# Queries and output gate of a hybrid block as block products, and where the branch gates' tiles run

## The chip, the cores and the metric

The kernel runs on one core of a Trainium2 chip. The core has TensorE for matrix products, VectorE and ScalarE for elementwise work, GpSimd (POOL) for elementwise work and for issuing transfers, SyncE (SP) for issuing transfers, and 16 DMA engines. Products land in PSUM, eight banks of 128 partitions x 512 float32. The metric is the device time of the core in microseconds; the time before is the median of three runs.

## The reference

One layer of a hybrid block on x of 512 tokens x 1024 features, in float32. Cut to what matters:

```python
h = rmsnorm(x, norm_mix_g)
gq, gk, gv, gr, glr, fq, fk, fv, ff, g_gla, g_fox = jnp.split(h @ w_in, IN_OFFSETS, axis=-1)
o_gla = gla_chunked(gq, gk, gv, log_a)                       # 4 heads, chunks of 64
o_gla = rmsnorm(o_gla, gla_out_norm_g) * jax.nn.silu(gr)     # output gate, 512 columns
o_fox = fox_attention(rmsnorm(fq), rmsnorm(fk), fv, log_f)   # 8 heads, queries 512 columns
y = sigmoid(g_gla + gate_b[0]) * (o_gla @ w_gla_branch) + sigmoid(g_fox + gate_b[1]) * (o_fox @ w_fox_branch)
x = x + y @ w_out
a, val = jnp.split(rmsnorm(x, norm_ffn_g) @ w_up, 2, axis=-1)
out = rmsnorm(x + (gelu(causal_dwconv(a)) * val) @ w_down)
```

Queries fq, keys fk, values fv and the output gate gr have 512 columns each, the gates g_gla (first) and g_fox (second) 1024 each.

## The kernel before

**Products.** Each float32 operand is split into a high part, rounded by ScalarE, and a low part, the difference, by VectorE (lines 293 and 294, one weight piece of 128 x 1024 each). `mm3` (lines 327 to 330) makes one product out of three on TensorE: high x high, high x low, low x high. Weights come in pieces of 512 KB, in the order of a list, `recipes`. `piece()` takes the next one; splits run three pieces ahead of TensorE (three buffers), loads up to four further, into places named raw, rawz, rawp or zr with two buffers each. SP issues the plain loads. A piece that is a sum of weight blocks is loaded first, and then another block is added to it by an accumulating transfer that POOL issues; `behind(n, ...)` names the split behind which a load, a sum or an addition is issued. Additions ("add") go into a place whose piece has just been split; "sum" is issued behind a one-column copy on POOL, `tick` (line 309).

**Block products.** Keys and values together (`fox_kv`, lines 737 to 787), the output projection and the MLP use a 2 x 2 block scheme with seven products for eight. `PAIR` (line 78) is its order: for each product p of 5, 1, 3, 6, 2, 7, 4 two pieces, each of 12 matmuls of 512 columns (two token tiles x two feature blocks x three). The left half of the result is the keys, the right half the values. `pair_done` combines the banks with ScalarE and VectorE, squares the keys and normalises them. The sums of activations that it multiplies with are made once (`pair_sums`, `pair_split`).

**Stages.** After a first stage (gated attention's q and k) come the gated attention's values. Then its small products are made; between them `fill(n)` takes n steps of a work list, so that TensorE has something while VectorE and ScalarE work. In this kernel the list holds `fox_q` (16 steps of 6 matmuls, token form) and `fox_kv` (28 steps of 6). `normalise` (lines 861 to 876) scales the gated attention's output by its norm, and transposes it, with a fill in each round.

Then comes the softmax attention. Its work list is `gates`: four tiles of the output gate gr (`zr`) and eight of the first branch gate (`zg`), each 24 matmuls in eight steps of three (`gate_tile`, line 927). `FRONT` and `RUNS` (lines 41 to 49) spread these 96 steps by hand between logits, transposes (t), values (v) and preparations of keys and queries (k).

Behind the attention the output gate's sigmoid, the product with it and with the gain, and the split into `ogh` and `ogl` run on ScalarE, GpSimd and VectorE (lines 1130 to 1139). The merge loop (lines 1142 to 1180) takes for each of eight column blocks c one tile of the second branch gate (`zf`, two blocks ahead, `GAHEAD`) and one branch piece: 12 matmuls for the gated branch, 12 for the attention branch. VectorE multiplies both with their gates, GpSimd adds them, and VectorE and ScalarE make the operands of the output projection's block products. Two pieces of that projection are split early and held (`HELD`). The MLP follows, and the second norm.

Beside this the weights of the down projection are combined in DRAM: copies (`COPY_AT`, issued on SP) and accumulating transfers (`ADD_AT`, on POOL) are hung behind chosen splits.

The instructions of each engine go in an order that a scheduler sets at build time: by program order, but an instruction whose operands are not ready by its estimate lets a later one pass; `issue_after` keeps an order.

## Time and profile before

| what | us |
|---|---|
| median of three runs (688.61, 690.53, 691.12) | 690.53 |
| the profiled execution | 688.75 |
| its span, first to last instruction | 687.0 |
| TensorE busy in the span | 680.2 |
| VectorE busy | 547.8 |
| ScalarE busy | 430.9 |
| GpSimd busy | 136.3 |

Busy time counts the instructions of an engine, not the time in which it waits; matmuls overlap, so their start-to-start distance tells more than their duration. In the rows of the profile PE is TensorE's matmuls, PEld its weight loads, DVE VectorE, ACT ScalarE, POOL GpSimd. A timeline row gives start, duration, engine, line, operation, output<-inputs, shape and count; a bracket gives the idle time before it and what ended it. A group row ends with busy time and mean duration in ns. In a row of transfers the last number is the median time from issue to landing in us.

### The profile page before, as it was taken

To read this page: it belongs to the slowest core of one execution; us is meant where nothing else is said; L and a number is where in the kernel's file an instruction comes from. 1 tells how busy PE (TensorE), PEld (TensorE's weight loads), DVE (VectorE), ACT (ScalarE), POOL (GpSimd) and SP (SyncE) were. 2 spreads that over 40 slices of the span, in tenths; PEclk is the share of its full clock that TensorE was granted. 3 is DMA by queue.
4 is the path that set the end of the run, shared out by engine and by line. 5 is a ranking of instruction groups with operands and counts; after the bars stand their busy time and mean duration, and the time that the engine had idled before them with its cause. 6 is when DMAs were issued, how large, how long until landed. Compare 5 with 4: busy or idle time off the path is not lost.

```text
span 687.0 us, 10636 instructions
## 1 busy us (share of the span) xinstructions
PE 680.2 (99%) x3875; PEld 585.4 (85%) x3875; DVE 547.8 (80%) x856; ACT 430.9 (63%) x698; POOL 136.3 (20%) x196
## 2 busy tenths in 40 slices
...
DMA  8769488989765489967975898999999988866643
GB/s 310 270 192 306 99 273 221 311 196 217 178 140 122 119 248 199 281 147 213 213 253 133 158 211 210 228 228 223 196 201 214 204 202 254 268 209 173 196 139 122
DMA packets 46184, 142.23 MB, mean 207 GB/s; under 512 B 5396, under 2 KB 9388, under 8 KB 46004
## 3 DMA queue, kind: packets, MB, share of 16 engines
q1 hardware_dynamic: 31156, 92.98, 40.3%
q0 software_dynamic: 11808, 43.52, 35.8%
...
## 4 chain that ended last, share of the span: by engine, by line
PE 99%; ACT 0%; issue 0%; DVE 0%; ACTq 0%
PE ps_mm L328 21%; PE ps_mm L330 20%; PE ps_mm L329 20%; PE ps_wide L1463 8%; PE ps_wide L328 5%; PE ps_wide L329 5%; PE ps_wide L330 5%; PE ps_wide L1465 4%; PE ps_lg L1042 1%; PE ps_lg L983 1%; PE ps_pt L1017 1%; PE ps_mm L490 1%; PE ps_ax L328 1%; PE ps_ax L330 1%; PE ps_ax L329 1%; PE ps_ax L378 1%
## 5 line engine op out<-in xcount | busy, mean ns | idle before, releaser
L293 ACT CAST wh<-rawx 128x1024 fp32r<-128x1024 f32 x75 | 76.0, 1013 | 61.5 <-PE ps_mm L329 30.9
L328 PE MATMUL ps_mm<-xw,wh 128*128 128x512 f32 (+1 forms) x320 | 109.4, 342 | 0.2 <-ACT wh L293 0.2
L329 PE MATMUL ps_mm<-xw,wh 128*128 128x512 f32 (+1 forms) x320 | 107.8, 337 | 0.0
L330 PE MATMUL ps_mm<-xw,wl 128*128 128x512 f32 (+1 forms) x320 | 107.6, 337 | 0.0
L294 DVE TENSOR_TENSOR wl<-rawx,wh 128x1024 fp32r<-128x1024 f32 x75 | 88.3, 1179 | 13.8 <-ACT wh L293 13.8
L294 DVE TENSOR_TENSOR wl<-raw,wh 128x1024 fp32r<-128x1024 f32 x58 | 74.6, 1287 | 9.7 <-ACT wh L293 9.4
L293 ACT CAST wh<-raw 128x1024 fp32r<-128x1024 f32 x58 | 60.7, 1049 | 32.0 <-PE ps_mm L329 20.2
L328 PEld LDWEIGHTS ps_mm<-xw,wh 128*128 128x128 f32 x320 | 60.8, 190 | 7.8 <-issue 1.2
L330 PEld LDWEIGHTS ps_mm<-xw,wl 128*128 128x128 f32 x320 | 60.8, 190 | 6.5
L329 PEld LDWEIGHTS ps_mm<-xw,wh 128*128 128x128 f32 x320 | 60.8, 190 | 5.9 <-DVE xw L1252 0.2
L294 DVE TENSOR_TENSOR wl<-rawz,wh 128x1024 fp32r<-128x1024 f32 x31 | 39.2, 1266 | 16.7 <-ACT wh L293 16.4
L1463 PE MATMUL ps_wide<-xo,wh 128*128 128x512 f32 x192 | 48.1, 392 | 0.0
L301 POOL DMA_DIRECT2D rawx<-in_wu_dram x30 | 25.9, 865 | 104.6 <-DVE wl L294 68.6
L328 PE MATMUL ps_mm<-xc,wh 128*128 128x256 f32 (+1 forms) x136 | 45.1, 332 | 0.0
L329 PE MATMUL ps_mm<-xc,wh 128*128 128x256 f32 (+1 forms) x136 | 44.6, 328 | 0.0
L330 PE MATMUL ps_mm<-xc,wl 128*128 128x256 f32 (+1 forms) x136 | 44.5, 327 | 0.0
L293 ACT CAST wh<-rawz 128x1024 fp32r<-128x1024 f32 x31 | 32.4, 1044 | 14.2 <-issue 5.0
L1463 PEld LDWEIGHTS ps_wide<-xo,wh 128*128 128x128 f32 x192 | 34.6, 189 | 6.2
L328 PE MATMUL ps_mm<-wh,xw 128*128 128x512 f32 x96 | 37.7, 393 | 0.0
L329 PE MATMUL ps_mm<-wl,xw 128*128 128x512 f32 x96 | 37.4, 390 | 0.0
L330 PE MATMUL ps_mm<-wh,xw 128*128 128x512 f32 x96 | 37.4, 390 | 0.0
L309 POOL COPY tick<-wl 128x1 f32<-128x1 f32 x37 | 10.6, 286 | 134.5 <-DVE wl L294 134.5
...
## 6 DMA issues: line engine op xcount, KB each, us to landing
rawx<-in_wu_dram POOLq DMA_DIRECT2D x40, 512.0 KB, 7.1
rawz<-in_wp_dram SPq DMA_DIRECT2D x30, 512.0 KB, 4.6
raw<-in_wp_dram SPq DMA_DIRECT2D x22, 512.0 KB, 5.1
wsum<-in_wd_dram SPq DMA_DIRECT2D x20, 512.0 KB, 6.3
rawx<-in_wu_dram SPq DMA_DIRECT2D x20, 512.0 KB, 4.9
raw<-in_wu_dram SPq DMA_DIRECT2D x20, 512.0 KB, 5.5
rawx<-wsum SPq DMA_DIRECT2D x12, 512.0 KB, 4.0
wsum<-in_wd_dram POOLq DMA_DIRECT2D x10, 512.0 KB, 8.2
```

Of the source, the lines that this page charges most:

```text
L293: nc.scalar.copy(out=hi[:, :m], in_=raw[:, :m])
L294: last_split[:] = [nc.vector.tensor_sub(out=lo[:, :m], in0=raw[:, :m], in1=hi[:, :m].bitcast(F32))]
L301: nc.gpsimd.dma_start(raw, recipes[i][0], accum_op=ALU.add)
L309: now = nc.gpsimd.tensor_copy(out=tick, in_=lo[:, 0:1].bitcast(F32))
L328: mm(ps, lhsT=ah, rhs=bh, start=start, stop=False, **k)
L329: mm(ps, lhsT=ah, rhs=bl, start=False, stop=False, **k)
L330: mm(ps, lhsT=al, rhs=bh, start=False, stop=stop, **k)
L378: mm(warm, lhsT=nc.const_aps.tensor(1.0, (P, P), BF16), rhs=nc.const_aps.tensor(1.0, (P, T), BF16), start=True, stop=True,)
L490: mm(first[i], lhsT=w[:, i * P : (i + 1) * P], rhs=x, start=(k == j == 0), stop=False)
L983: last = mm(lg[:, place_of_q(qb)], lhsT=a[r, q], rhs=b[r, :n], start=(j == 0), stop=(j == 2))
L1463: mm(ps[:, i], lhsT=wh[:, c], rhs=both[p][:, k], start=first and k == 0, stop=False, skip_group_check=True)
L1465: mm(ps[:, i, 0], lhsT=wl[:, c], rhs=both[p][:, k, 0], start=False, stop=k == KH - 1, skip_group_check=True,)
```

## The change

Queries and output gate become the left and right half of a second run of the block scheme: `fox_kv` becomes `pair_stage` with its destinations as arguments, run first for keys and values and then, with the other places for its pieces, for queries (`qf`) and output gate (`gz`). `fox_q` and the four output gate tiles of the attention go. As the gate is now in token form, its sigmoid and products (`silu`) run behind products 2 and 4 of that stage, in front of the transposes (`transpose_heads`), whose evacuation takes the gain; the split into `ogh` and `ogl` stays behind the attention.

In the place of `fox_q`, four tiles of the first branch gate run between the gated attention's products. They are stored to DRAM and loaded again in front of the merge loop. The other four and all eight of the second gate form the attention's work list, again 96 steps, of which `RUNS` and `FRONT` now take 88 and the last `fill()` eight. The merge loop has only branch pieces.

Copies and sums of the down weights hang behind other splits, six sums behind splits of the last stage, and the load and sum of the output projection's first product behind other branch pieces. Lines that only rename or carry the new arguments are left out.

```diff
-    (6, "k1", 2, "t0", 6, "t1"),
-    (7, "t2", 4, "v0", 3, "t3"),
-    (6, "k2", 2, "t4", 6, "t5"),
-    (6, "v1", 1, "t6", 3, "k3", 4, "t7"),
-    (7, "t8", 4, "v2", 3, "t9"),
-    (8, "t10", 6, "t11", 4, "v3"),
+    (6, "k1", 2, "t0", 5, "t1"),
+    (7, "t2", 3, "v0", 3, "t3"),
+    (6, "k2", 2, "t4", 5, "t5"),
+    (6, "v1", 1, "t6", 3, "k3", 3, "t7"),
+    (7, "t8", 3, "v2", 3, "t9"),
+    (8, "t10", 5, "t11", 2, "v3"),
...
-GAHEAD = 2
+NEARLY = 4
...
-COPY_AT = [10 + i for i in range(24)]
-ADD_AT = [32 + i if i < 10 else 42 + (i - 10) * 20 // 14 for i in range(24)]
+COPY_AT = [8 + i * 2 // 3 for i in range(18)] + [44 + 2 * i for i in range(6)]
+ADD_AT = [44 + i for i in range(12)] + [56 + i * 3 // 2 for i in range(6)]
+LATE_ADDS = 6
...
-OSUM = (1, 3)
+OSUM = (4, 5)
...
-    parts_at(ADD_AT, adds_at, ((0, b11), (2, b12), (1, wsum[0]), (3, wsum[1])))
+    parts_at(ADD_AT, adds_at, ((0, b11), (2, b12), (1, wsum[0])))
...
-    at_pair = {}
-    for p, r in PAIR:
-        k11, k21, k12, k22 = (wps[i + r] for i in (12, 14, 8, 10))
-        new, before, place = {
-            1: (k11, None, "rawz"), 2: (k21, None, "rawz"), 3: (k22, None, "rawp"), 7: (k12, 3, None),
-            5: (k12, None, "raw"), 6: (k22, 5, None), 4: (k21, 6, None),
-        }[p]
-        at_pair[p, r] = len(recipes)
-        recipes.append((new, at_pair[before, r] if before else None, 1024, place))
+    def pair_recipes(a, b, places):
+        at = {}
+        for p, r in PAIR:
+            k11, k21, k12, k22 = (wps[i + r] for i in (a, a + 2, b, b + 2))
+            new, before, place = {
+                1: (k11, None, places[0]), 2: (k21, None, places[0]), 3: (k22, None, places[1]), 7: (k12, 3, None),
+                5: (k12, None, places[2]), 6: (k22, 5, None), 4: (k21, 6, None),
+            }[p]
+            at[p, r] = len(recipes)
+            recipes.append((new, at[before, r] if before else None, 1024, place))
+        return at
+    at_kv = pair_recipes(16, 12, ("rawz", "rawp", "raw"))
+    at_qr = pair_recipes(20, 8, ("rawz", "raw", "rawp"))
...
-    n_out = 16 + GH + 3 * KD
+    n_gate = 24
+    n_out = n_gate + 3 * KD - NEARLY
...
-        behind(KD + 1, "load", at_pair[5, r])
-        behind(KD + 3 + r, "sum", at_pair[5, r], at_pair[1, r])
-        for p, q in ((5, 6), (3, 7), (6, 4)):
-            behind(at_pair[p, r], "add", at_pair[q, r])
+        behind(KD + 1, "load", at_kv[5, r])
+        behind(KD + 3 + r, "sum", at_kv[5, r], at_kv[1, r])
+        behind(at_kv[7, r], "load", at_qr[5, r])
+        behind(at_kv[2, 1] + r, "sum", at_qr[5, r], at_qr[1, r])
+        for at in (at_kv, at_qr):
+            for p, q in ((5, 6), (3, 7), (6, 4)):
+                behind(at[p, r], "add", at[q, r])
         for p, q in ((5, 6), (3, 7), (6, 4)):
             behind(at_out[p, r], "add", at_out[q, r])
-        behind(at_branch[OSUM[0] + r], "load", at_out[5, r])
-        behind(at_branch[OSUM[1] + r], "sum", at_out[5, r], at_out[1, r])
+        behind(at_branch[OSUM[0] + 2 * r], "load", at_out[5, r])
+        behind(at_branch[OSUM[1] + 2 * r], "sum", at_out[5, r], at_out[1, r])
...
+    parts_at([at_last[1 + i] for i in range(LATE_ADDS)], adds_at, ((3, wsum[1]),))
...
-    def fox_q():
-        ssq = gpool.tile([P, NT, FH], F32, name="qssq")
-        def done(tt, ps):
-            nc.scalar.activation(out=qf[:, tt, :], in_=ps, func=AF.Copy, scale=rt[:, tt : tt + 1])
-            squares(qf, ssq, tt)
-        yield from token_group(xh, xl, done)
-        qk_norm(qf, ssq, range(NT))
+    def gate_tile(put):
+        ps = pmm()
+        wh, wl = piece()
+        for k in range(KD):
+            c = slice(k * P, (k + 1) * P)
+            mm3(ps, wh[:, c], wl[:, c], xh[k], xl[k], k == 0, k == KD - 1)
+            yield
+        put(ps)
+    def put_early(i):
+        def put(ps):
+            z = gpool.tile([P, T], F32, tag="sq", name="early", bufs=2)
+            nc.vector.tensor_mul(out=z, in0=ps, in1=rb)
+            nc.sync.dma_start(early[:, i], z)
+        return put
...
-    def fox_kv():
-        ssq = gpool.tile([P, NT, FH], F32, name="kssq")
+    def pair_stage(ssq, left, right, final=lambda tt: None):
...
                 if r == 1:
-                    pair_done(p, t2, ps, ssq)
+                    pair_done(p, t2, ps, ssq, left, right, final)
                 yield
...
-            scaled(vf[:, 2 + t2], 2 + t2)
+            scaled(right[:, 2 + t2], 2 + t2)
+            final(2 + t2)
...
-    work += [fox_q(), fox_kv()]
-    fill(4)
-    gpool.tile([P, 72], F32, name="padg")
+    qssq, kssq = (gpool.tile([P, NT, FH], F32, name=f"{c}ssq") for c in "qk")
+    work += [gate_tile(put_early(i)) for i in range(NEARLY)] + [pair_stage(kssq, kf, vf)]
+    fill(8)
...
-    fill(2)
+    fill(4)
...
-    fill(4)
+    fill(8)
...
-        fill(2)
+        fill(4 if tt < NT - 1 else 2)
...
-    def normalise(u, obs):
+    def silu(tt):
+        sg = gpool.tile([P, 512], F32, tag="sq", name="sg", bufs=2)
+        nc.scalar.activation(out=sg, in_=gz[:, tt], func=AF.Sigmoid)
+        nc.gpsimd.tensor_mul(out=sg, in0=gz[:, tt], in1=sg)
+        nc.vector.tensor_mul(out=ons[:, tt], in0=ons[:, tt], in1=sg)
+    def transpose_heads(u):
         for par in range(2):
-            on = gpool.tile([P, 4, GDV], F32, tag="sq", name="on", bufs=2)
-            nc.vector.tensor_mul(
-                out=on, in0=obs[par].rearrange("p (a v) -> p a v", v=GDV),
-                in1=rg[:, u * 8 + par * 4 : u * 8 + par * 4 + 4].unsqueeze(2).broadcast_to([P, 4, GDV]),
-            )
-            fill(4)
             pt = pax()
-            for a in range(4):
-                nc.tensor.transpose(pt[:, a * P : (a + 1) * P], on[:, a, :], ident)
+            for t2 in range(2):
+                for j in range(2):
+                    a, h = 2 * t2 + j, 2 * j + par
+                    nc.tensor.transpose(
+                        pt[:, a * P : (a + 1) * P], ons[:, 2 * u + t2, h * GDV : (h + 1) * GDV], ident
+                    )
             for j in range(2):
-                nc.scalar.copy(
-                    out=ogr[2 * j + par][:, 2 * u * P : 2 * (u + 1) * P].rearrange("p (t l) -> p t l", l=P),
-                    in_=pt.rearrange("p (t j l) -> p t j l", j=2, l=P)[:, :, j, :],
+                h = 2 * j + par
+                nc.scalar.activation(
+                    out=ogr[h][:, 2 * u * P : 2 * (u + 1) * P].rearrange("p (t l) -> p t l", l=P),
+                    in_=pt.rearrange("p (t j l) -> p t j l", j=2, l=P)[:, :, j, :], func=AF.Copy, scale=col(C_OG + h),
                 )
...
+    ons = gpool.tile([P, NT, 512], F32, tag="prev", name="ons")
     for u in range(2):
-        normalise(u, obs[u])
+        for par in range(2):
+            g = u * 8 + par * 4
+            nc.vector.tensor_mul(
+                out=ons[:, 2 * u : 2 * u + 2].rearrange("p t (j e v) -> p t j e v", e=2, v=GDV)[:, :, :, par],
+                in0=obs[u][par].rearrange("p (t j v) -> p t j v", j=2, v=GDV),
+                in1=rg[:, g : g + 4].rearrange("p (t j) -> p t j", j=2).unsqueeze(3).broadcast_to([P, 2, 2, GDV]),
+            )
+    gz = gpool.tile([P, NT, 512], F32, tag="vg", name="gz")
+    work += [pair_stage(qssq, qf, gz, silu)]
     fill()
+    for u in range(2):
+        transpose_heads(u)
...
-    zr = [zrs[i // 2][:, i % 2 * T : (i % 2 + 1) * T] for i in range(GH)]
     raw_pools["zr"] = gtpool
-    zg = [gtpool.tile([P, T], F32, tag="zg", name=f"zg{i}", bufs=KD) for i in range(KD)]
-    def gate_tile(z):
-        ps = pmm()
-        wh, wl = piece()
-        for k in range(KD):
-            c = slice(k * P, (k + 1) * P)
-            mm3(ps, wh[:, c], wl[:, c], xh[k], xl[k], k == 0, k == KD - 1)
-            yield
-        nc.vector.tensor_mul(out=z, in0=ps, in1=rb)
-    gates = [gate_tile(z) for z in zr + zg]
+    zs = [gtpool.tile([P, T], F32, tag="zg", name=f"zg{i}", bufs=KD) for i in range(KD)]
+    zg = {NEARLY + i: zs[i] for i in range(4)}
+    zf = {i: zrs[i // 2][:, i % 2 * T : (i % 2 + 1) * T] for i in range(4)}
+    zf.update({4 + i: zs[4 + i] for i in range(4)})
+    def put_in(z):
+        return lambda ps: nc.vector.tensor_mul(out=z, in0=ps, in1=rb)
+    gates = [gate_tile(put_in(z)) for z in [zg[c] for c in range(NEARLY, KD)] + [zf[c] for c in range(KD)]]
...
+    for i in range(NEARLY):
+        zg[i] = bpool.tile([P, T], F32, tag="zd", name="zd", bufs=NEARLY)
+        nc.sync.dma_start(zg[i], early[:, i])
     for h in range(GH):
-        sg = bpool.tile([P, T], F32, tag="sg", name="sg", bufs=2)
-        sigmoid(zr[h], sg)
-        nc.gpsimd.tensor_mul(out=zr[h], in0=zr[h], in1=sg)
-        nc.vector.scalar_tensor_tensor(
-            out=zr[h], in0=ogr[h], scalar=col(C_OG + h), in1=zr[h], op0=ALU.mult, op1=ALU.mult
+        nc.scalar.copy(out=ogh[h], in_=ogr[h])
+        ogl.append(
+            zpool.tile([P, T], F32R, tag="og", name=f"ogl{h}", bufs=GH) if h else held_place[:, 4 * 1024 : 4 * 1024 + T]
         )
-        nc.scalar.copy(out=ogh[h], in_=zr[h])
-        ogl.append(zpool.tile([P, T], F32R, tag="og", name=f"ogl{h}", bufs=GH))
-        nc.vector.tensor_sub(out=ogl[h], in0=zr[h], in1=ogh[h].bitcast(F32))
-    zf = {}
+        nc.vector.tensor_sub(out=ogl[h], in0=ogr[h], in1=ogh[h].bitcast(F32))
     held = []
-    for c in range(-GAHEAD, KD):
-        if c + GAHEAD < KD:
-            zf[c + GAHEAD] = bpool.tile([P, T], F32, tag="zf", name="zf", bufs=GAHEAD + 1)
-            for _ in gate_tile(zf[c + GAHEAD]):
-                pass
-        if c < 0:
-            continue
+    for c in range(KD):
         w = piece()
...
-    for name in ("gv", "fq", "fk", "fv"):
+    gg, gf = ([by_feature(cols(name, D), c) for c in range(KD)] for name in ("gg", "gf"))
+    for name in ("gv", "fq", "fk", "fv", "gr"):
         ps += [by_token(cols(name, 512), i) for i in range(4)]
-    ps += [by_feature(cols("gr", 512), c) for c in range(GH)]
-    ps += [by_feature(cols("gg", D), c) for c in range(KD)]
-    for c in range(-GAHEAD, KD):
-        if c + GAHEAD < KD:
-            ps.append(by_feature(cols("gf", D), c + GAHEAD))
-        if c < 0:
-            continue
+        if name == "gv":
+            ps += gg[:NEARLY]
+    ps += gg[NEARLY:] + gf
+    for c in range(KD):
```

38 lines of the change are left out of this document (18 added, 20 removed).

## The prediction

> **What bounds the kernel now.** I read the page's busy line and chain first, then TensorE's own timeline to see whether "busy" hides waiting, then a table by stage.
>
> ```profile
> span 687.0 us, 10636 instructions
> PE 680.2 (99%) x3875; PEld 585.4 (85%) x3875; DVE 547.8 (80%) x856; ACT 430.9 (63%) x698; POOL 136.3 (20%) x196
> DMA  8769488989765489967975898999999988866643
> PE 99%; ACT 0%; issue 0%; DVE 0%; ACTq 0%
> ```
>
> The chain that ended last is TensorE nearly throughout, so time is won only by giving TensorE less, and lost only where something makes it wait. A busy TensorE may still wait inside its busy time, so the starts are what to look at:
>
> ```profile
> 48.12 0.39 PE L328 MATMUL ps_ax<-wh,xc 128*128 128x512 f32 x1
> ...
> 58.77 0.39 PE L330 MATMUL ps_mm<-wh,xw 128*128 128x512 f32 x1
> ...
> 80.59 0.39 PE L328 MATMUL ps_mm<-wh,htz 128*128 128x512 f32 x1
> ...
> 83.09 0.39 PE L330 MATMUL ps_mm<-wh,lmz 128*128 128x512 f32 x1
> ...
> 126.38 0.39 PE L328 MATMUL ps_mm<-xw,wh 128*128 128x512 f32 x1
> ...
> 128.87 0.39 PE L330 MATMUL ps_mm<-xw,wl 128*128 128x512 f32 x1
> ```
>
> These are three runs without other work: 48 token products in 47 steps of 10.65/47 = 0.2266 us, 12 block products (2.50/11 = 0.227) and 12 feature products (2.49/11 = 0.226). All three forms that the change trades go at 0.2267 us each, with no gap. So what TensorE gets is a row of 512-column products, and each that is dropped is worth 0.2267 us, if it isn't given back as a wait.
>
> ```profile
> 80.50:126.30 45.80, 45.80 (x282) 38.52 (x281) 41.30 (x89) 31.15 (x72) 4.27 (x5) 1.00 0.83 239
> 126.30:224.80 98.50, 98.50 (x562) 81.85 (x560) 70.58 (x178) 72.59 (x164) 24.34 (x48) 1.00 0.77 188
> 241.20:312.00 70.80, 70.80 (x314) 58.63 (x314) 49.11 (x65) 27.46 (x38) 25.70 (x35) 1.00 0.88 217
> ```
>
> The stages are: keys and values with the gated attention's end, the softmax attention, the merge loop (columns: PE, PEld, DVE, ACT, POOL, clock, DMA share). VectorE is at 41.3 of 45.8 us (90%) in the first, the DMA engines at 0.83 to 0.88 in the outer two: these are what could become late.
>
> **The change part by part.**
>
> *Products.* Queries took 4 pieces x 4 token tiles x 6 = 96 products, the output gate 4 tiles x 24 = 96. The block form takes 14 pieces x 2 x 6 = 168. The transposes (16) and all gate tiles are only moved. So 24 products go: 24 x 0.2267 = **-5.44 us** on TensorE, the whole of the possible gain.
>
> ```profile
> L328 PEld LDWEIGHTS ps_mm<-xw,wh 128*128 128x128 f32 x320 | 60.8, 190 | 7.8 <-issue 1.2
> ```
>
> A weight load takes 0.190 us, under the 0.2267 us step. [...] The starts above speak for the full step.
>
> *Six more pieces* (14 for 8), each converted by ScalarE and VectorE, and eight more accumulating transfers:
>
> ```profile
> L293 ACT CAST wh<-rawz 128x1024 fp32r<-128x1024 f32 x31 | 32.4, 1044 | 14.2 <-issue 5.0
> L294 DVE TENSOR_TENSOR wl<-raw,wh 128x1024 fp32r<-128x1024 f32 x58 | 74.6, 1287 | 9.7 <-ACT wh L293 9.4
> q1 hardware_dynamic: 31156, 92.98, 40.3%
> q0 software_dynamic: 11808, 43.52, 35.8%
> raw<-in_wp_dram POOLq DMA_DIRECT2D x6, 512.0 KB, 8.7
> rawp<-in_wp_dram POOLq DMA_DIRECT2D x2, 512.0 KB, 7.0
> 130.42 0.84 POOL L311 DMA_DIRECT2D wsum<-in_wd_dram  x1 [0.20 <-issue]
> ```
>
> That is 6 x 1.04 us of ScalarE and 6 x 1.29 us of VectorE beside TensorE. A block piece gives TensorE 12 x 0.2267 = 2.72 us, so both keep up, as they do in the keys' stage. From the queue rows a 512 KB plain load costs the 16 engines 1.56 us (40.3% of 687 over 92.98 MB) and an accumulating one 2.96 us. Keys and the new stage together (28 pieces, about 82 us with what lies between) ask for some 14 of each, 63 us: 0.77, less than the 0.83 now, since most copies of the down weights now come before and their sums after.
> The tight place is the **start of the new stage**. Its first piece is loaded behind the split of the keys' product 7 and summed behind that of the last product 2, three pieces before it is needed. Split 27 ends 1.04 + 1.29 = 2.33 us after its buffer is free; piece 30 may be split 3 x 2.72 = 8.16 us after that buffer, and without harm as late as 5.44 - 2.33 = 3.1 us more. The window is 8.9 us; needed are about 0.5 (the tick), 0.84 and a landing of 7.0 to 8.7: 8.3 to 10.0. So 0 to 1.1 us of waiting, up to twice that if its load is late too. I take 0.3.
>
> *Second gate's tiles.* Eight move from the merge loop into the attention, the four early ones of the first gate leave it for the place of the queries, and four output gate tiles are gone from it: 12 before, 12 after, 96 steps each. So the attention's cover is the same but for 8 steps kept for its end. The early four go through DRAM: four stores and four loads of 256 KB on SP. A store waits for its tile's VectorE product with later loads behind it, but these wait for buffers two tiles on. The reloads are due only at the first merge product. Nothing, or a few tenths if that cover goes.
>
> *Output gate's sigmoid* moves into the new stage, with two more table loads (Sigmoid before the attention's Exp, then back).
>
> ```profile
> L1128 ACT ACTIVATE sg<-zr x4: 615/625/634, 229.5 to 232.8; 128x512 f32<-128x512 f32 x4
> L1133 POOL TENSOR_TENSOR zr<-zr,sg x4: 1285/1512/1742, 230.2 to 234.4; 128x512 f32<-128x512 f32 x4
> L1128 ACT ACT_TABLE_LOAD  x1: 1283/1283/1283, 220.5 to 220.5; - x1
> ```
>
> Two loads are 2.6 us of ScalarE, which has 14.6 us free in the keys' stage. I count nothing. [...]
> **The end of the new stage** is where VectorE is late:
>
> ```profile
> 127.41 1.29 DVE L674 TENSOR_TENSOR kf<-kf,rq 128x512 f32<-128x512 f32 x2
> 129.10 0.60 PE L946 MATMUL ps_lg<-ident,kf 128*128 128x128 f32 x4
> 132.80 0.33 PE L983 MATMUL ps_lg<-kh,qh 64*128 64x128 f32 x2
> 269.56 2.24 DVE L294 TENSOR_TENSOR wl<-raw,wh 128x1024 fp32r<-128x1024 f32 x1 [0.21 <-ACT wh L293]
> 269.44 1.29 POOL L1161 TENSOR_TENSOR zg<-zf,zg 128x512 f32<-128x512 f32 x1 [0.65 <-DVE zf L1158]
> ```
>
> Now the keys' norm ends at 128.7, 2.3 us after TensorE left the stage (126.38) and 0.4 us before its transposes. The queries take that place and bring four 512-wide products (0.68 each, as L1158 below) and four on GpSimd; beside one of these a split took 2.24 instead of 1.29. So 2.7 to 6.5 us more: the norm ends 5.0 to 8.8 us behind the stage, the first logits' operands some 1.9 later, 6.9 to 10.7. TensorE has till then 24 gate products (5.44), 16 moved transposes and 8 others (24 x 0.11 = 2.6): 8.0 us, if the scheduler puts gate products ahead of transposes that wait. It does such things:
>
> ```profile
> 31.15 0.48 PE L328 MATMUL ps_ax<-wh,xw 128*128 128x512 f32 x1
> ...
> 34.22 0.39 PE L329 MATMUL ps_ax<-wl,xw 128*128 128x512 f32 x1
> 34.44 0.40 PE L328 MATMUL ps_mm<-wh,xw 128*128 128x512 f32 x1
> ...
> 37.65 0.39 PE L330 MATMUL ps_ax<-wh,xw 128*128 128x512 f32 x1
> ```
>
> The program asks for 12 products into ps_ax and then ps_mm; 14 ran first, two of the next piece while ps_mm's bank was not free. So 0 to 2.7 us; I take 0.5.
>
> *End of the attention.* After the last values TensorE had 72 gate products before the merge; now 24 (5.44 us). But the sigmoid, GpSimd and VectorE chain in front of the first operand is gone; left are a cast and a difference (0.62 + 0.69) that need nothing of the attention. Nothing; 0.5 if they queue badly.
>
> *Merge loop.* Each step gave TensorE 48 products, now 24: 5.44 us. VectorE must keep that pace. The last two steps of before already ran so:
>
> ```profile
> 301.30 0.69 DVE L1158 TENSOR_TENSOR zf<-ps_mm,zf 128x512 f32<-128x512 f32 x1 [2.03 <-PE ps_mm L330]
> 306.54 0.39 PE L328 MATMUL ps_mm<-ogh,wh 128*128 128x512 f32 x1
> 307.52 0.68 DVE L1158 TENSOR_TENSOR zf<-ps_mm,zf 128x512 f32<-128x512 f32 x1
> 311.98 0.39 PE L328 MATMUL ps_mm<-held,oh 128*128 128x512 f32 x1
> 313.98 0.68 DVE L1158 TENSOR_TENSOR zf<-ps_mm,zf 128x512 f32<-128x512 f32 x1
> 317.93 0.68 DVE L1121 TENSOR_TENSOR ol<-zg,oh 128x512 fp32r<-128x512 f32 x1
> 320.14 0.39 PE L328 MATMUL ps_mm<-wh,oh 128*128 128x512 f32 x1
> ```
>
> VectorE takes a step's second product 1.0 us late at step 6 and 2.0 at step 7: a cycle of 6.2 to 6.5 us against 5.44. The operand that it makes last ends at 318.6, for 320.14: 1.5 us to spare. Now steps 4 and 5 go at that pace too (+1.0 each), with two held pieces to split (2 x 1.29): 2.0 to 4.6 us more lateness, so 0.5 to 3.1 us of waiting; part of it may be filled by other products, as above. I take 0.8. *Six sums of down weights* (6 x 2.96 = 18 us of DMA) move into the end, where the DMA line falls to 8, 6 and 4: nothing, 1 us at most.
>
> **Sum:** -5.44 + 0.3 + 0.5 + 0.8 = -3.84. The profiled execution took 688.75 (span 687.0 and 1.75 around it), so 684.9 of its kind; it was a quick one of its runs, and by the median 690.53 the time is **686.7**.
>
> **The rivals.** (1) *All covered*: the waits are filled, 690.53 - 5.44 = 685.1. For it: not one gap now, even with 0.4 us to spare. Against: VectorE at 90%. It and the forecast lie on one side of the bound below (-5.4 to -3.5): 0.2 for it, 0.35 for the forecast. (2) *VectorE takes the gain back* at the end of the new stage and of the merge loop, with the first pieces late: 1.1 + 2.7 + 3.1 = 6.9 at its worst, 691.9; at its middle, 3.5, 688.6. Chance 0.39. (3) *The merge loop becomes VectorE's*: every step waits for one serial chain with GpSimd's addition in it. Two steps' PSUM banks give about 8.2 us of slack, so eight steps cost 8 x (cycle - 5.44) - 8.2: nothing is left of the gain at a cycle of 7.1 us, and at 7.8 (6.5 and one more split of 1.29 in each step) the waits are 10.7, so 695.8. Against it: 6.5 is the longest seen, and steps 0 to 3 have less work. Chance 0.06.
>
> About 0.5% (3.45 us) is what a measurement of this kernel can tell from no change. Faster by more needs under 2.0 us of waits: 0.55; within: 0.39; slower: 0.06. The range goes from 684.2 (all covered, and 0.9 for the spread of medians) to 690.8 (waits of 5.7).
>
> **What would show it.** 24 matmuls fewer (3851 but for records missing); three starts in a row still 0.2267 apart; a gap on TensorE before the new stage's first products (line of the block pieces), before the first logits, and before the second half of output product 5. Wrong would be gaps elsewhere: a piece waiting for its transfer inside the new stage, TensorE waiting in the merge steps, or the end's loads late.

## The result, and the profile after

The changed kernel takes 723.0 us (median of 4 runs, 720.45 to 725.04) against 689.57 for the kernel before: a ratio of 1.0481, 95% interval 1.0439 to 1.0524. It is 4.8% slower; the prediction, 686.7 in a range of 684.2 to 690.8, has the wrong sign. The profiled execution took 720.45.

The page of the changed kernel, its busy line, DMA line and the chain that ended last:

```profile
span 718.7 us, 10670 instructions
PE 686.5 (96%) x3851; PEld 583.1 (81%) x3851; DVE 553.7 (77%) x876; ACT 442.2 (62%) x712; POOL 153.5 (21%) x206
DMA  8789959875767767687895689999999988986543
PE 68%; DVE 10%; DMA 9%; ACT 8%; issue 3%; POOL 2%; DVEq 0%; ACTq 0%; POOLq 0%
```

The 24 matmuls are gone, as promised. But the chain, 99% TensorE before, is 68% TensorE now: a third of its length leads through other engines. That is not the time lost, which is counted below; it says that TensorE waits in many places. TensorE is also *longer* busy with less to do (686.5 us for 680.2), since waits and slow stretches count as busy: 32.2 us of the span are not busy, and the waits counted below come to 54.8. Four stages (keys and start of the new stage; its rest; attention; merge loop. Columns: PE, PEld, DVE, ACT, POOL, clock, DMA share, GB/s):

```profile
83.40:137.20 53.80, 49.60 (x286) 40.52 (x285) 38.09 (x75) 30.13 (x64) 7.24 (x10) 1.00 0.75 179
137.20:183.70 46.50, 39.65 (x185) 32.30 (x183) 36.92 (x59) 28.58 (x42) 12.58 (x14) 1.00 0.71 183
183.70:275.70 92.00, 89.51 (x505) 73.78 (x506) 61.27 (x164) 66.77 (x155) 22.47 (x44) 0.98 0.71 180
281.40:329.80 48.40, 45.19 (x192) 35.60 (x192) 29.00 (x48) 22.01 (x35) 17.24 (x19) 1.00 0.79 208
```

No engine is full where time is lost: VectorE is at 36.9 of 46.5 us, where before it had 41.3 of 45.8 without a wait, and the DMA share in the keys' stage, the attention and the merge loop is lower than before (0.75, 0.71 and 0.79 for 0.83, 0.77 and 0.88). So the loss looks like waiting for *order*, not like lack of room; the experiments test it. To locate it, TensorE's starts were taken one by one, and from each interval the step of 0.2267 us per 512 columns was subtracted. What is left over is its **waits** (a transpose of 128 columns took 0.108 us, four from 129.10 to 129.53 in the kernel before, where a quarter of the step is 0.057; the attention has 3.7 in the kernel before too). All kernels are cut at the same products:

| us of waits beyond the step | keys, start of new stage | to first logits | attention | merge loop | output to first wide | end |
|---|---|---|---|---|---|---|
| before | 1.3 | 0.5 | 3.7 | 0.0 | 2.4 | 0.9 |
| changed | 5.7 | 9.6 | 8.3 | 5.2 | 7.5 | 9.4 |

With 9.2 before and 9.1 after in the stretches not shown (the start and the wide products), that is 18.0 and 54.8. The rest is work: 687.0 - 18.0 = 669.0 and 718.7 - 54.8 = 663.9, so 5.1 us less. The saving is there; 36.8 us of waits stand against it, and 36.8 - 5.1 = 31.7 is the difference of the spans. The places, in order of time. First the start of the new stage (timeline rows of SyncE, GpSimd, ScalarE, VectorE and TensorE: start, duration, and in brackets the idle time before and what ended it):

```profile
109.13 3.98 SPq L269 DMA_DIRECT2D rawp<-in_wp_dram  x2
...
115.95 0.85 POOL L316 DMA_DIRECT2D rawp<-in_wp_dram  x1 [1.05 <-DMA rawp<-in_wp_dram]
117.93 0.86 POOL L316 DMA_DIRECT2D rawp<-in_wp_dram  x1 [0.35 <-issue]
...
124.54 1.05 ACT L298 CAST wh<-rawp 128x1024 fp32r<-128x1024 f32 x1 [2.94 <-DMA rawp<-in_wp_dram]
...
126.96 0.50 PE L334 MATMUL ps_mm<-wl,htz 128*128 128x512 f32 x1 [0.81 <-DVE wl L299]
...
129.50 1.23 DVE L299 TENSOR_TENSOR wl<-rawp,wh 128x1024 fp32r<-128x1024 f32 x1 [2.52 <-ACT wh L298]
...
134.15 2.36 DVE L299 TENSOR_TENSOR wl<-rawz,wh 128x1024 fp32r<-128x1024 f32 x2
...
135.43 0.50 PE L334 MATMUL ps_mm<-wl,xw 128*128 128x512 f32 x1 [1.63 <-DVE wl L299]
```

The first piece's load could go out at 109.13, when its buffer was free; it landed 6.8 us later, and only then could GpSimd issue the sum, which took 8.6 more. TensorE stood still for it, 1.09 us beyond the step, and 0.97 for the second piece of product 5. The longest wait, 1.79 at 135.43, is ahead of product 1, whose piece is a plain load. Its split starts on VectorE at 134.15: VectorE had stood 2.52 us for product 5's second piece, and the end of the keys' norm came in between. The end of the same stage:

```profile
171.91 0.17 DVE L377 SCALAR_TENSOR_TENSOR rq<-rq16w,rq 128x16 f32<-128x16 f32 x1
...
172.33 3.23 DVE L376 TENSOR_TENSOR rq16w<-rq16w,rq16v 128x16 f32<-128x16 f32 x1
...
172.71 2.81 POOL L873 TENSOR_TENSOR sg<-gz,sg 128x512 f32<-128x512 f32 x2
...
178.48 1.17 PE L882 MATMUL ps_ax<-ident,ons 128*128 128x128 f32 x8 [3.27 <-DVE ons L874]
...
183.71 0.33 PE L1004 MATMUL ps_lg<-kh,qh 64*128 64x128 f32 x2 [1.56 <-ACT qh L979]
...
187.57 0.63 PE L333 MATMUL ps_mm<-xw,wh 128*128 128x512 f32 x1
188.00 0.63 PE L334 MATMUL ps_mm<-xw,wh 128*128 128x512 f32 x1
```

VectorE's step of the norm, 0.17 us elsewhere, takes 3.23 beside two products of GpSimd; TensorE has the waiting transposes at the head of its queue; and behind the waits it goes at 0.43 us a step for a while (the granted clock was 0.50 from 187.5 to 190.0). In the attention, about 1 us twice: a split of weights stands on VectorE just ahead of the probabilities' low halves (`pl`). The first of the two, rows of VectorE and TensorE:

```profile
208.22 1.23 DVE L299 TENSOR_TENSOR wl<-rawz,wh 128x1024 fp32r<-128x1024 f32 x1 [1.87 <-ACT wh L298]
209.37 1.28 DVE L1045 TENSOR_TENSOR pl<-ps_pt,ph 128x512 fp32r<-128x512 f32 x2
...
210.11 0.50 PE L1063 MATMUL ps_lg<-pl,v 128*128 128x512 f32 x1 [0.89 <-DVE pl L1045]
```

Then the merge loop (GpSimd, VectorE, TensorE):

```profile
305.61 0.18 POOL L314 COPY tick<-wl 128x1 f32<-128x1 f32 x1
312.55 0.90 POOL L316 DMA_DIRECT2D zr<-in_wp_dram  x1 [6.76 <-DMA zr<-in_wp_dram]
...
313.83 1.91 POOL L1174 TENSOR_TENSOR zd<-zr,zd 128x512 f32<-128x512 f32 x1
...
316.22 0.42 DVE L1142 TENSOR_TENSOR ol<-zd,oh 128x256 fp32r<-128x256 f32 x1 [6.66 <-ACT oh L1141]
...
317.73 0.47 PE L333 MATMUL ps_mm<-ogh,wh 128*128 128x512 f32 x1 [1.27 <-DVE zg L1170]
```

The first GpSimd row is the marker that every sum of weights carries; behind it GpSimd stands 6.76 us at a sum whose load has not landed. The addition of step 3, ready since 308.4, is behind it; VectorE waits 6.66 us for what follows from that addition, and the product that would free TensorE's bank is behind *that*. Last, the end (TensorE's first product of that stage, then GpSimd, VectorE, TensorE):

```profile
592.76 0.40 PE L333 MATMUL ps_wide<-wh,acth 128*128 128x512 f32 x1
...
606.08 7.54 POOL L314 COPY tick<-wl 128x1 f32<-128x1 f32 x1
613.57 0.58 POOL L316 DMA_DIRECT2D xo<-x2d  x1
...
622.39 1.29 DVE L1674 TENSOR_TENSOR xo<-xo,ps_wide 128x512 f32<-128x512 f32 x2 [5.49 <-DMA xo<-x2d]
...
624.87 0.80 PE L334 MATMUL ps_mm<-wl,xw 128*128 128x512 f32 x1 [3.71 <-DVE wl L299]
```

The reload of the kept rows is issued at 613.57, 20.8 us after the last stage's first product (592.76), behind three of the six sums and a marker of 7.54 us. VectorE stands 5.49 us for it, with the next split behind. In the kernel before it was issued 6.7 us after that product:

```profile
569.95 0.40 PE L328 MATMUL ps_wide<-wh,acth 128*128 128x512 f32 x1
...
576.62 0.56 POOL L311 DMA_DIRECT2D xo<-x2d  x1
```

### The profile page after: what moved, and what is told of

It is laid out like the page before. It is cut to its first block, busy times and chain, and to the rows that moved or that the text cites. A ratio compares the mean times of both kernels' runs of the same rounds, so it can differ in the third digit from the quotient of the medians.

```text
span 718.7 us, 10670 instructions
## 1 busy us (share of the span) xinstructions
PE 686.5 (96%) x3851; PEld 583.1 (81%) x3851; DVE 553.7 (77%) x876; ACT 442.2 (62%) x712; POOL 153.5 (21%) x206
## 4 chain that ended last, share of the span: by engine, by line
PE 68%; DVE 10%; DMA 9%; ACT 8%; issue 3%; POOL 2%; DVEq 0%; ACTq 0%; POOLq 0%
PE ps_mm L334 12%; PE ps_mm L333 12%; PE ps_mm L335 12%; PE ps_wide L1476 8%; PE ps_wide L1478 4%; PE ps_wide L333 4%; PE ps_wide L335 4%; PE ps_wide L334 4%; DMA zr<-in_wp_dram 4%; DVE wl L299 4%; ACT wh L298 2%; DMA early<-early 2%; DMA rawp<-in_wp_dram 1%; ACT pr L1016 1%; DMA xo<-x2d 1%
## 5 line engine op out<-in xcount | busy, mean ns | idle before, releaser
L333 PE MATMUL ps_mm<-xw,wh 128*128 128x256 f32 (+1 forms) x296 | 101.0, 341 | 0.1
L334 PE MATMUL ps_mm<-xw,wh 128*128 128x256 f32 (+1 forms) x296 | 99.2, 335 | 0.0
L335 PE MATMUL ps_mm<-xw,wl 128*128 128x256 f32 (+1 forms) x296 | 99.1, 335 | 0.0
L299 DVE TENSOR_TENSOR wl<-raw,wh 128x1024 fp32r<-128x1024 f32 x58 | 71.4, 1233 | 11.6 <-ACT wh L298 10.6
L333 PEld LDWEIGHTS ps_mm<-xw,wh 128*128 128x128 f32 x296 | 56.7, 192 | 7.4 <-issue 1.4
L335 PEld LDWEIGHTS ps_mm<-xw,wl 128*128 128x128 f32 x296 | 56.7, 191 | 5.6
L334 PEld LDWEIGHTS ps_mm<-xw,wh 128*128 128x128 f32 x296 | 56.7, 192 | 5.1 <-DVE xw L1265 0.2
L334 PE MATMUL ps_mm<-wl,xw 128*128 128x512 f32 x88 | 35.8, 407 | 6.8 <-DVE wl L299 6.8
L333 PE MATMUL ps_mm<-xc,wh 128*128 128x256 f32 (+1 forms) x128 | 42.0, 328 | 0.0
L334 PE MATMUL ps_mm<-xc,wh 128*128 128x256 f32 (+1 forms) x128 | 41.5, 324 | 0.0
L335 PE MATMUL ps_mm<-xc,wl 128*128 128x256 f32 (+1 forms) x128 | 41.4, 324 | 0.0
L314 POOL COPY tick<-wl 128x1 f32<-128x1 f32 x38 | 19.8, 520 | 100.4 <-DVE wl L299 98.0
L335 PE MATMUL ps_mm<-wh,xw 128*128 128x512 f32 x88 | 35.3, 401 | 0.0
L333 PE MATMUL ps_mm<-wh,xw 128*128 128x512 f32 x88 | 35.1, 400 | 0.0
```

What stands on the lines that cost most here:

```text
L299: last_split[:] = [nc.vector.tensor_sub(out=lo[:, :m], in0=raw[:, :m], in1=hi[:, :m].bitcast(F32))]
L314: now = nc.gpsimd.tensor_copy(out=tick, in_=lo[:, 0:1].bitcast(F32))
L333: mm(ps, lhsT=ah, rhs=bh, start=start, stop=False, **k)
L334: mm(ps, lhsT=ah, rhs=bl, start=False, stop=False, **k)
L335: mm(ps, lhsT=al, rhs=bh, start=False, stop=stop, **k)
```

## The experiments

Three theories. **Q**: single items of the in-order queues stand ahead of work that is due; each wait is local. **D**: transfers crowd each other. **V**: VectorE has more to do than time. Each kernel is the changed one (or, once, the one before) with the edit shown. Places where nothing was edited scatter from kernel to kernel by about 2 us, at the start and in the attention by up to 3.6. A smaller step in one column is not read by itself, unless a row shows the wait. The merge column begins with the wait for the first merge operand. All waits together:

| us of waits | keys, start | to logits | attention | merge | output | end | time | ratio to before |
|---|---|---|---|---|---|---|---|---|
| before | 1.3 | 0.5 | 3.7 | 0.0 | 2.4 | 0.9 | 689 | |
| changed | 5.7 | 9.6 | 8.3 | 5.2 | 7.5 | 9.4 | 723.0 | 1.048 |
| no_sums | 4.8 | 7.4 | 6.5 | 2.5 | 3.0 | 0.9 | 700.8 | 1.018 |
| xo_sp | 3.8 | 11.1 | 10.1 | 4.2 | 9.5 | 0.9 | 715.6 | 1.038 |
| late_alone | 1.6 | 0.2 | 3.8 | 0.0 | 2.4 | 8.3 | 696.8 | 1.010 |
| order | 0.5 | 6.4 | 6.9 | 5.3 | 9.4 | 7.7 | 711.3 | 1.032 |
| silu_dve | 4.3 | 3.4 | 8.5 | 5.1 | 9.1 | 8.3 | 713.9 | 1.037 |
| osum | 4.5 | 9.7 | 11.7 | 2.6 | 5.5 | 7.5 | 717.9 | 1.040 |
| merge_dve | 7.4 | 8.8 | 9.1 | 2.5 | 5.8 | 7.2 | 717.9 | 1.040 |
| runs | 5.7 | 8.8 | 15.5 | 1.8 | 4.8 | 8.3 | 720.7 | 1.046 |
| three | 2.4 | 6.0 | 8.5 | 4.9 | 7.7 | 0.9 | 704.0 | 1.021 |
| best1 | 1.2 | 5.3 | 8.5 | 2.0 | 4.6 | 1.0 | 697.4 | 1.012 |
| best2 | 1.0 | 6.4 | 6.6 | 5.2 | 4.2 | 1.4 | 699.4 | 1.015 |
| best3 | 0.7 | 4.0 | 6.0 | 2.0 | 4.6 | 0.9 | 693.8 | 1.008 |
| best4 | 2.3 | 4.5 | 3.8 | 1.7 | 3.8 | 2.8 | 692.3 | 1.006 |
| best5 | 1.3 | 4.4 | 3.9 | 1.7 | 4.0 | 0.9 | 690.5 | 1.003 |
| best6 | 0.4 | 4.4 | 3.9 | 1.7 | 3.6 | 0.9 | 690.2 | 1.003 |
| best7 | 0.4 | 1.7 | 4.9 | 1.7 | 3.5 | 0.9 | 688.8 | 0.999 |

**The end: three runs.** First without any sum of down weights:

```diff
-    parts_at(ADD_AT, adds_at, ((0, b11), (2, b12), (1, wsum[0])))
-    parts_at([at_last[1 + i] for i in range(LATE_ADDS)], adds_at, ((3, wsum[1]),))
```

> The changed kernel without any of its 24 accumulating transfers into the down weights' sums (left out: the additions; the copies stay, so the output misses the summed blocks). In the changed kernel TensorE waits, beyond its cadence, 5.8 us from 83 us to the end of the keys' stage (before: 1.4), 8.9 to the first logits (0.5), 9.0 in the attention (3.7), 4.9 in the merge loop (0), 7.5 from the output product to the first wide product (2.4) and 9.4 in the end (0.9). Theory Q, in-order queues: single items of GpSimd's and VectorE's queues stand ahead of work that is due, and only where a sum is that item is a wait cured: the end falls to about 1, merge loop and output products lose about half (6), the two stages before the attention keep theirs: 708 to 712 us. Theory D, crowded transfers: 71 us of DMA time (24 x 2.96) are gone, all loads land as before the change and most of the 37 us come back: under 700. Theory V, VectorE has too much work: its work stays, so only the end gets better: 714 to 718.

700.8 us (the output then lacks the summed blocks), better than Q's figure and close to D's: 22 us hang on the sums, 8.5 in the end and 7.2 in merge and output. D would have wanted both stages ahead of the attention cured too; they keep 12.2 of 15.3. But this run takes away GpSimd's queue items and their transfers at once. The next keeps every transfer and moves two off the queue:

```diff
-    dma_behind(last_lo, x2t, x2d)
-    dma_behind(last_lo, fgt, fing.broadcast_to([P, D]))
+    nc.sync.dma_start(x2t, x2d)
+    nc.sync.dma_start(fgt, fing.broadcast_to([P, D]))
```

> The changed kernel with the two reloads that the end needs (the kept rows and the last gain) issued by SyncE instead of GpSimd, where they stood behind late sums. The sums stay where they are. Theory Q: the 9.4 us of waiting in the end fall to 1 to 3, the rest stays: about 716. Theory D: the reload lands late anyway since the sums fill the transfers: 9.4 stays over 6, 720 or more.

The end's 9.4 are 0.9, with all six sums in place: Q. The timeline of this run (SyncE, GpSimd, VectorE):

```profile
593.47 0.44 SPq L1591 DMA_DIRECT2D xo<-x2d  x1
...
610.91 6.73 POOL L314 COPY tick<-wl 128x1 f32<-128x1 f32 x1 [1.07 <-DVE wl L299]
...
615.70 1.89 DVE L1400 TENSOR_TENSOR actl<-act,acth 128x512 fp32r<-128x512 f32 x3
617.67 1.23 DVE L299 TENSOR_TENSOR wl<-rawx,wh 128x1024 fp32r<-128x1024 f32 x1
```

The reload goes out at 593.47, and GpSimd's slow marker (6.73 us for one element a partition) now holds up a sum only. Then the part alone, in the kernel before:

```diff
-    parts_at(ADD_AT, adds_at, ((0, b11), (2, b12), (1, wsum[0]), (3, wsum[1])))
+    parts_at(ADD_AT[:18], adds_at, ((0, b11), (2, b12), (1, wsum[0])))
...
+    parts_at([at_last[1 + i] for i in range(6)], adds_at, ((3, wsum[1]),))
```

> The kernel before with one part of the change alone: its last six sums of down weights are ordered behind the splits of the second to seventh last-stage pieces, as in the changed kernel, so they stand in GpSimd's queue around the end's two reloads. Theory Q: the reloads are issued 10 us or more later than now (576.6 us) and the end gets 6 to 9 us of waits (0.9 now); 696 to 699, as much as in the changed kernel, though nothing else is changed. Theory D (in the changed kernel the end is late because everything before it crowds the transfers): under 2 us, 690 to 692.

696.8 against 689.3: 7.4 us for moving six sums, nothing else, and all of it in the end (8.3 for 0.9). The same marker and the same reload (GpSimd and VectorE):

```profile
583.21 7.27 POOL L311 COPY tick<-wl 128x1 f32<-128x1 f32 x1
590.43 0.58 POOL L313 DMA_DIRECT2D xo<-x2d  x1
...
599.29 1.28 DVE L1663 TENSOR_TENSOR xo<-xo,ps_wide 128x512 f32<-128x512 f32 x2 [5.53 <-DMA xo<-x2d]
```

**The new stage: two runs.** Its products in another order (`PAIR_QR` is used for its recipes and its products):

```diff
+PAIR_QR = tuple((p, r) for p in (1, 5, 2, 3, 6, 7, 4) for r in range(2))
```

> The changed kernel with the new block stage's products in the order 1, 5, 2, 3, 6, 7, 4 for 5, 1, 3, 6, 2, 7, 4 (and banks to match): its first two pieces are plain loads, and the two summed pieces are due 5.4 us later. Theory Q: the load of 6.8 us and the sum of 8.6 us behind the release of one buffer are the wait at the stage's start: 5.8 us there fall to about 2, and the gate's tiles for the first half are ready earlier: 717 to 720. Theory D: all transfers of the stage are late, so the wait moves to products 6 or 7: 721 to 724.

0.5 us are left at the start, and 3.2 go at the end of the stage as well, as expected from product 2, and with it the gate of the first half, coming earlier. Q; 711.3 is better than its figure.

```diff
-        nc.gpsimd.tensor_mul(out=sg, in0=gz[:, tt], in1=sg)
+        nc.vector.tensor_mul(out=sg, in0=gz[:, tt], in1=sg)
```

> The changed kernel with the four 128x512 products of the output gate with its sigmoid on VectorE instead of GpSimd. Theory Q with its port form (GpSimd's products hold VectorE up: 3.23 us for an instruction that takes 0.17 elsewhere, 2.40 for two of 0.65): of the 8.9 us of waiting before the first logits 3 to 5 go, and the slow clock behind it: 717 to 720. Theory V: 4 x 0.68 = 2.7 us more for VectorE just where it is late: 8.9 becomes 10 to 12, 724 to 727.

9.6 fall to 3.4 although VectorE has four more products. V would have made it worse: it is GpSimd's part, not VectorE's amount of work. The slowed step is gone (0.16 us at that place), but so are GpSimd's products of 1.41 to 1.74 us, 0.68 on VectorE, from the chain; the run doesn't part the two. The expectation calls this the port form; what holds VectorE up beside GpSimd's products, no run shows.

**The merge loop: two runs.** `osum` orders product 5's sums behind product 2's splits, and takes product 5 third:

```diff
-        behind(at_branch[OSUM[1] + 2 * r], "sum", at_out[5, r], at_out[1, r])
+        behind(at_out[2, r], "sum", at_out[5, r], at_out[1, r])
-OUT = (1, 5, 2, 3, 6, 7, 4)
+OUT = (1, 2, 5, 3, 6, 7, 4)
```

> The changed kernel with the output projection's product 5 taken third instead of second, and its two sums ordered behind the merge additions of steps 4 and 5 on GpSimd (in the changed kernel the sum of its first piece stood ahead of the addition of step 3, and waited from 305.8 to 312.6 us for the load before it). Theory Q: the merge loop's waits fall from 4.9 us to 1 to 2 and those from the output product to the first wide product from 7.5 to 3 to 4; 715 to 718. Theory V (VectorE's work of a step is over TensorE's 5.44 us): they stay over 4 and 6, 721 or more. Theory D: the loads of product 5 still take 6 to 11 us and the wait moves to that product, 720 or more.

Merge and output go from 12.7 to 8.1: 4.6 for Q. They are still 5.7 over the kernel before. Nearly all of the merge loop's 2.6 stands at its first step, where TensorE waits for `ogl` (as in the changed kernel, where it is 2.5); the rest of the loop has none. Another 2.5 stand ahead of product 5. First a row of that step in the changed kernel, then rows of this run (VectorE, ScalarE, TensorE):

```profile
286.00 0.51 PE L334 MATMUL ps_mm<-ogl,wh 128*128 128x512 f32 x1 [0.52 <-DVE ogl L1159]
```

```profile
322.36 1.22 DVE L299 TENSOR_TENSOR wl<-raw,wh 128x1024 fp32r<-128x1024 f32 x1
...
324.75 0.43 DVE L1183 TENSOR_TENSOR zd<-zg,zd 128x256 f32<-128x256 f32 x1 [1.18 <-POOL zg L1181]
...
328.82 1.21 DVE L299 TENSOR_TENSOR wl<-raw,wh 128x1024 fp32r<-128x1024 f32 x1
...
341.05 2.01 ACT L298 CAST wh<-zr 128x1024 fp32r<-128x1024 f32 x2
...
342.16 0.51 PE L333 MATMUL ps_mm<-wh,oh 128*128 128x512 f32 x1 [1.33 <-ACT wh L298]
```

VectorE's splits come 6.46 us from one to the next, where TensorE needs 5.44. That is the pace the prediction took (6.2 to 6.5). But VectorE isn't full: it stands 1.18 us of each such step for GpSimd's addition. The pace is that of a chain through both engines, not of VectorE's amount of work. It costs nothing inside the loop of this run. Where it shows is behind it: ScalarE casts product 5's weights behind the loop's last operands and the copies of product 1's result. In `best4` below the copies come later, and these waits go. So the pace is there, as V has it, but its cause isn't VectorE's amount of work. The second run:

```diff
-            nc.gpsimd.tensor_add(out=y, in0=z, in1=y)
+            nc.vector.tensor_add(out=y, in0=z, in1=y)
-            nc.gpsimd.tensor_add(out=z, in0=z, in1=zg[c])
+            nc.vector.tensor_add(out=z, in0=z, in1=zg[c])
```

> The changed kernel with the merge loop's eight additions on VectorE instead of GpSimd; the sums of product 5 stay where they are. Theory Q: no computing is left behind GpSimd's waiting transfers, so the merge loop's 4.9 us fall to about 1 though VectorE gets 8 x 0.68 = 5.4 us more; about 718. Theory V: the loop gets slower by up to 5 us, 724 to 729.

The same 8.3 in merge and output, though VectorE has eight more instructions and the sums stay where they are. Taking the computing out from behind the transfer is worth as much as taking the transfer away (it takes GpSimd out of the step's chain, too).

**The attention's table** gets back the steps that the changed kernel keeps for the end (one pair of rows of `RUNS`; the others likewise, 8 steps in all):

```diff
-    (7, "t2", 3, "v0", 3, "t3"),
+    (7, "t2", 4, "v0", 3, "t3"),
...
-    (8, "t10", 5, "t11", 2, "v3"),
+    (8, "t10", 6, "t11", 4, "v3"),
```

> The changed kernel with the attention's table of gate products as it was before the change (88 steps of three products inside it, none kept for its end). Theory Q: the attention's 8.3 us of waits (3.7 before the change; 1.4 of the rest is the slow clock behind the earlier gap) come from splits that stand on VectorE ahead of the probabilities' low halves, which the table only shifts: 7 to 9 stays, and the attention's end gets 2 to 4 us of waits, 724 to 727. A rival, cover: the attention lost the 8 steps as cover: its waits fall to about 5, and the end pays less than that: 719 to 722.

The two waits at the values are gone, but TensorE then waits 7.17 us in one piece for the first merge operand (the table counts it in the attention here):

```profile
287.41 0.80 PE L333 MATMUL ps_mm<-ogh,wh 128*128 128x512 f32 x1 [7.17 <-ACT ogh L1155]
```

Q had the place wrong, since the waits at the values go, and both guesses had the end too cheap. In sum the waits only shift: merge and output get 6.1 shorter, and the time is that of the changed kernel within the noise (1.0431 to 1.0496 against 1.0439 to 1.0524). Whether the eight steps are better kept for the end isn't shown.

**Together.** The edits of `order`, `silu_dve` and `xo_sp`:

> The changed kernel with three edits together: the new stage's products in the order 1, 5, 2, 3, 6, 7, 4, the output gate's products with its sigmoid on VectorE, and the end's reloads issued by SyncE. Theory Q: the waits are local, so the gains add: start and end of the new stage 15.3 to 3, the end 9.4 to 1, the rest as in the changed kernel; 700 to 704. Theory D or V: a wait removed turns up at a later place, and the sum is less than half of the singles' (7.4, 9.1, 11.7 us): over 708.

704.0, the edge of Q's figure and far from D's and V's. The gains of the singles, 11.7, 9.1 and 7.4, make 28.2; 19.0 came. They don't simply add: start and end of the new stage keep 8.4, where Q had 3. Two of the edits act on the same waits to the first logits, which is part of the reason. Next, `osum` with them, and two steps of the attention's table:

```diff
-    (7, "t2", 3, "v0", 3, "t3"),
+    (7, "t2", 4, "v0", 3, "t3"),
...
-    (7, "t8", 3, "v2", 3, "t9"),
+    (7, "t8", 4, "v2", 3, "t9"),
```

> The three edits of the earlier run (704.0 us) and two more: product 5 of the output projection third, with its sums behind the merge additions; and two steps of gate products given back to the attention where its values waited for a split that VectorE took first (3 to 4 ahead of the first and the third values). Theory Q: 2.6 + 2.0 us in merge and output as measured alone, and 2.2 us of the two waits at the values: 696 to 699. Theory V: the merge loop goes at VectorE's pace of 6.46 us a step, so the wait comes back at the output products: 700 to 703.

697.4, as Q says. Merge goes from 4.9 to 2.0, all of it at the first step; of the output's 5.3 over the kernel before, 2.2 stay. The two waits at the values shrink (1.05 and 1.15 to 0.40 and 0.60), but the attention's column doesn't. A miss was to take cover from the attention's end:

```diff
-FRONT = (4, 4)
+FRONT = (6, 4)
+        with tc.issue_after(last_norm[0].ins):
             nc.vector.tensor_mul(out=sg, in0=gz[:, tt], in1=sg)
             nc.vector.tensor_mul(out=ons[:, tt], in0=ons[:, tt], in1=sg)
```

> The same with two edits at the end of the new block stage: the last silu products on VectorE are ordered behind the queries' norm (they stood between its parts), and two steps of gate products more are put ahead of the first logits, taken from those kept for the attention's end. Theory Q: of some 3.5 us of waits before the first logits and 1.4 of slow clock behind them, 3 to 4 go, and the attention's end loses 1 at most: 693 to 696. Cover as the rival: what is taken from the attention's end costs as much there: 697 to 699.

699.4, worse. The logits' wait did not fall (6.4), and the first merge operand comes 2 us later (3.44 for 1.47, in the merge column): the rival was right. The amount of work at that place was tried next, on top of `best1`:

```diff
-        nc.scalar.activation(out=sg, in_=gz[:, tt], func=AF.Sigmoid)
-        nc.vector.tensor_mul(out=sg, in0=gz[:, tt], in1=sg)
+        nc.scalar.activation(out=sg, in_=gz[:, tt], func=AF.Silu)
```

> The five edits of the run at 697.4 us and one more: ScalarE applies silu in one instruction, so VectorE loses the four products of the output gate with its sigmoid (4 x 0.68 us), two of which stand in the chain of the last queries' norm. Theory V for this one place (what is left of the waits at the end of the new stage, 4.8 us over those before the change, is VectorE's own work between the last product and the first logits): 1.5 to 3 us go, slow clock included; 694.5 to 696. Theory Q (the order of the queues alone): the last transposes and the norm's small steps set it, under 0.7 us go: 696.7 to 697.5.

693.8, V's figure and more: 1.3 us go at the logits and 2.5 in the attention behind them. The edit takes work off VectorE and a link out of the chain at once, so that it is the amount alone is not shown. Then order alone again: transposes behind a product of the stage, gate steps in the table, sigmoids behind the last copy of a merge operand, the additions of product 1 behind product 2:

```diff
-    (6, "k1", 2, "t0", 5, "t1"),
+    (6, "k1", 2, "t0", 6, "t1"),
...
-    (8, "t10", 5, "t11", 2, "v3"),
+    (7, "t10", 5, "t11", 2, "v3"),
...
+                    with tc.issue_after(stage_mm[(7, 0, 1) if u == 0 else (4, 1, 1)].ins):
...
+            last_copy[:] = [ogh_copy]
...
+    accx = [pax(), pax()]
+    out_product(2, accx)
```

> The version at 693.8 us with four edits that change the order of instructions alone, none of them an engine or an amount of work: the transposes of the gated heads are put on TensorE behind product 7 and product 4 of the new stage; two steps of gate products are moved so that no tile of weights is split just ahead of the values; the merge loop's sigmoids from step 4 on come behind the casts of the gated heads; the copies of product 1's result come behind product 2, so that product 5's splits do not stand behind them on ScalarE. Waits left over those before the change: 3.5 us at the end of the new stage, 2.3 in the attention, 1.6 at its end, 2.6 in merge and output. Theory Q: 3 to 4 us of these 10 go: 690 to 691. Theory V (VectorE's and ScalarE's work between the stages sets what is left, in whatever order): under 1 us, 693 to 694.

692.3, between both, and its interval (1.0035 to 1.0085) overlaps that of `best3` (1.0064 to 1.0099). The attention is at 3.8, as before the change, the wait for the first merge operand goes from 1.5 to 0.3, and the waits ahead of product 5 go (output 4.6 to 3.8). Start and end are higher in this profile (2.3 and 2.8). Then the transfers, in two runs:

```diff
-    parts_at([at_last[1 + i] for i in range(LATE_ADDS)], adds_at, ((3, wsum[1]),))
+    parts_at([at_last[10 + 3 * i] for i in range(LATE_ADDS)], adds_at, ((3, wsum[1]),))
```

> The version at 692.3 us with the six late sums spread out: behind every third last-stage piece from the eleventh on, for the second to seventh. In the profile of the version at 692.3 the end waits 2.8 us (0.9 before the change) since a piece of the last stage lands late (589.6 us) among three sums. Theory D, for this place: the sums crowd the end's loads, so 1.5 to 2 us go: 690.3 to 691. Theory Q: the end's waits were the order of GpSimd's queue alone, which is cured by then, and the 2.8 is one execution's scatter: under 0.7, 691.6 to 692.5.

```diff
-COPY_AT = [8 + i * 2 // 3 for i in range(18)] + [44 + 2 * i for i in range(6)]
+COPY_AT = [8 + i for i in range(18)] + [44 + 2 * i for i in range(6)]
```

> The same, and the first 18 copies of down weights one behind each split from the eighth on, for three behind two. The first gate's early tiles are stored in that stretch, and VectorE waits for their store (0.7 us in the changed kernel, 1.2 in the version at 692.3), and TensorE for VectorE (1.2 and 2.1 us at the chunk products). Theory D: these go, about 1 to 2 us, and the copies that move into the keys' stage cost less than that: 689 to 690.5. Theory Q: no change, or the start of the new stage gets its loads later: 690.5 to 693.

The first gives 690.5, D's figure, and the end goes from 2.8 to 0.9. But `xo_sp`, `three`, `best1` and `best3` have the six sums where `best4` has them, and 0.9 to 1.0 in the end, and the intervals overlap: that the 2.8 was one execution's scatter is not ruled out. The copies make no difference that can be told (690.2, intervals 1.0019 to 1.0043 and 1.0016 to 1.0040). Last, the order of products once more, and with it the transposes of the first half behind product 4, which the expectation doesn't name:

```diff
-PAIR_QR = tuple((p, r) for p in (1, 5, 2, 3, 6, 7, 4) for r in range(2))
+PAIR_QR = PAIR[2:4] + PAIR[:2] + PAIR[4:]
-                    banks.setdefault(name, []).append(pmm())
+                    banks.setdefault(name, []).append((pax if name == "y" and order is PAIR_QR else pmm)())
-                    with tc.issue_after(stage_mm[(7, 0, 1) if u == 0 else (4, 1, 1)].ins):
+                    with tc.issue_after(stage_mm[(4, 0, 1) if u == 0 else (4, 1, 1)].ins):
```

> The version at 690.2 us with the new stage's products in the order of the keys' stage again, but for 1 and 5, which stay swapped, and with the bank of the third sum taken from the four that the chunk products have left. In the version at 690.2 TensorE waits 1.80 us ahead of product 7, since it follows product 6 at once and VectorE's two passes over product 6 (1.29 and 1.40 us for both tiles) lie between them; here half of product 2 stands between. Theory V, for this place: VectorE's two passes are covered, so 1.5 to 1.8 us go: 688.3 to 689. Theory Q: the wait moves to another instruction of the same chain (the last norm starts as late): 690 to 690.5.

688.8, ratio 0.9991 (0.9978 to 1.0005): the 1.80 us are gone, the waits to the logits go from 4.4 to 1.7, and the change is as fast as the kernel before, not faster. Waits are 22.6 against 18.0; the 4.6 between them eat the 5.1 saved.

## Why the prediction was wrong

The prediction put three terms of waiting into its sum, 0.3 + 0.5 + 0.8 = 1.6 us, and everything else at nothing. 36.8 us were measured.

*Right.* The saving: 24 matmuls fewer, 5.1 us of work less for 5.44. The pace of the merge loop's chain: 6.46 for 6.2 to 6.5. That the new stage itself keeps up once it runs, and that it is weak at its start and its end. That a busy TensorE may hide waits: 96% busy, with 54.8 us of them.

*The step that failed most*: "Six sums of down weights ... move into the end, where the DMA line falls to 8, 6 and 4: nothing, 1 us at most." It priced a transfer by the room that the DMA engines have, and that room was there: with the six sums in place and the reloads issued by SyncE the end waits 0.9 us (`xo_sp`), as before the change. It did not ask what else stands in the queue that issues it. The reloads of the end do. Price: 8.5 us in the changed kernel, 7.4 alone. Among its signs of being wrong stood "the end's loads late".

*Start of the new stage*, 0.3 taken, 2.2 the far end, 4.4 measured. The place and the first cause were right, and product 5's two pieces cost 2.06 us (1.09 + 0.97), inside the far end: the sum took 8.6 us for 7.0 to 8.7, and its load was late too. What the sum left out is what stands behind a late piece on VectorE: the keys' norm, and the split of product 1, 1.79 us more.

*End of the new stage*, 0.5 taken, 2.7 the far end, 9.1 measured. VectorE's lateness was nearly right: the norm ended 9.7 us behind the stage's last product (177.73 against 168.02), for 5.0 to 8.8. From there to the first logits it took 6.0 us; the prediction had 1.9 to their operands. The prediction let TensorE run gate products in that time; but the transposes of the gated heads, which it counted as cover, themselves wait for the products of GpSimd and VectorE and stand ahead in TensorE's queue. What was named as cover was a part of the late chain.

*Attention*: no price, 4.6 measured. 2.2 of it is the two waits at the values, where the gate steps shifted against the tiles; about 1.4 is the slow clock behind the waits before (seven steps of 0.43 us for 0.2267). The rest is open.

*Merge loop*, 0.8 taken, 3.1 the far end, 10.3 with the output projection. 4.6 of it (`osum`; 4.4 by `merge_dve`) is GpSimd's queue with a sum ahead of an addition, which the prediction did not look at. 2.5 stand at the first step, where the operands `ogl` come late: the prediction had that under the end of the attention, at nothing, 0.5 if they queue badly. 2.5 stand ahead of product 5, behind the chain's pace, inside the 0.5 to 3.1 that it foresaw. The chain is the one its third rival names, with GpSimd's addition in it, at 6.46 us a step and not at the 7.1 at which this rival takes the whole gain.

*The rival* "VectorE takes the gain back" had the places but not the means. In none of them did the amount of VectorE's work decide until the queues were mended (`silu_dve`, `merge_dve` gave it more and were faster); then an edit that took work off it helped (`best3`), where amount and chain are not told apart. What is left in `best7`, 4.6 us, lies by the table in the logits, the attention, merge and output, 1 to 2 us each; it was not taken apart further.
